# Hybrid attention and recurrence layer on one core: four instead of five of x's chunks turned on PE, the first stage in one written table of moves, the squares later, two weight copies merged

## The chip, the cores and the metric

The kernel runs on one core of one Trainium2 chip. The metric is the device time of one execution in microseconds (us), here the median of three runs. A core has five engines that each work through a row of instructions of their own in order: PE (matrix products), DVE (elementwise), ACT (elementwise with a function), POOL (a slower elementwise engine, and DMAs started by software) and SP, which in this kernel only starts DMAs. An engine waits for another by semaphores.

## The reference

One layer on x of 512 tokens x 2048 features, float32:

```python
def hybrid_layer(x, norm_w, w_in, ...):
    h = rms_norm(x, norm_w)
    proj = jnp.einsum('bsd,de->bse', h, w_in)            # 2048 -> 4608
    q, k, v, g_attn, xr, g_lru = jnp.split(proj, SPLITS, axis=-1)
    attn_out = attention_group(q, k, v, q_norm_w, k_norm_w)   # 8 heads, 2 for k and v, axial rope
    lru_out = lru_group(xr, conv_w, conv_b, ...)              # conv of 4 taps, gates, scan both ways
    mixed = jnp.concatenate([rms_norm(attn_out, attn_norm_w) * jax.nn.silu(g_attn),
                             rms_norm(lru_out, lru_norm_w) * jax.nn.silu(g_lru)], axis=-1)
    return x + jnp.einsum('bse,ed->bsd', mixed, w_out)
```

Each product is made in float32 accuracy from split operands: a high part (a cast) and a low part (the rest), three matmuls high x high, high x low and low x high.

## The kernel before, in words

All matrix work is matmuls of 128 x 128 weights with 512 columns. A projection takes 512 output columns at a time and runs over w_in in eight chunks of 256 rows: a chunk is one load `wr` of 512 KB (L206, by SP), two casts on ACT into `wh` (L218) and two subtractions on DVE into `wl` (L219), and 24 matmuls on PE (L153 to L155; L388 in the first chunks). In the text a chunk of the first stage is c=0 to c=7 and its weights w0 to w7.

The **first stage** projects the first half of the LRU input while x itself comes in: x also has eight chunks (256 features of all tokens, 512 KB), and PE needs each with the features on the partitions. Before, chunks 0 to 4 are turned by PE (`xturn`, L253, eight 128 x 128 transposes a chunk, then scaled and split by ACT and DVE). Chunks 5 to 7 go the other way: DVE turns blocks of 32 x 32 (`blocks`, L281), SP writes them to DRAM (`put_aside`, L289, here called D), reads them back in four pieces with the blocks in their places (`bring_back`, L296, called R), and ACT and DVE scale and split them (L338, L339, called V). Each chunk is also squared for the norm (`xsquare`): by DVE for the turned chunks (L272), by ACT for the others (L268).

Behind it come the second half of the LRU input, K and V together, two halves of Q, attention, the gates and the output product, with the recurrence woven between the projections. Where the text speaks of them: `hs` are the results of the recurrence (L558), their squares `hsq` (L567, one buffer) are added into `hsum` on DVE (L568); K, V (`kv`) and the Q tiles (`ev`) are evacuated by ACT (L596), their squares for the head norm (`sh`) are summed by ACT (L608), the root is taken by POOL, and DVE applies norm and rope (L613 to L622). K and Q are also turned by DVE blocks through DRAM (`uq` to `qd` to `lq`), K into `kt`.

What sets the order: PE's row is written by hand throughout. In the first stage SP's row is as well, and ACT's and DVE's until step (1, 2) (chunk 1, output tile 2); behind that, a scheduler places the instructions of ACT, DVE and SP by their priorities (`high_priority(AHEAD)`: as if written 600 instructions sooner) and by when it takes their operands to be ready. `moves` names what each step of the first stage brings, `issue_after` holds an instruction behind another. SP's row is one queue: what waits there holds up what stands behind.

Of the kernel before, what the change touches and what calls it, by code (L numbers as in the profile page):

```python
# [11 lines left out]
F32 = mybir.dt.float32  # L12
# [5 lines left out]
P = 128  # L18
# [31 lines left out]


B = 32
TURNED = 5
NQ = P // B


# [7 lines left out]
def hybrid_kernel(  # L64
# [53 lines left out]
    def nm(s):  # L118
        cnt[0] += 1
        return f"{s}_{cnt[0]}"  # L120
# [28 lines left out]
    def f(ap):  # L149
        return ap.bitcast(F32)  # L150
# [78 lines left out]

    xh, xl = [None] * KT, [None] * KT  # L230
    ssq = const([P, NT, KT // 2], "ssq")
    highs, x_parts, squared = {}, [], []

    def xload(c, nk=1):

        xc = b4(shape=(P, NT, 2 * P))
        for k in range(nk):
            ks = slice(k * 2 * P // nk, (k + 1) * 2 * P // nk)
            cs = slice(c * 2 * P + ks.start, c * 2 * P + ks.stop)
            nc.sync.dma_start(xc[:, :, ks], xf[:, cs].rearrange("(t p) d -> p t d", p=P))  # L240
            yield xc

    def behind(those):
        stack = ExitStack()
        for ins in those:
            stack.enter_context(tc.issue_after(ins))
        return stack

    def xturn(xc, kk, then=None):
        pt = mm()  # L250
        for t in range(NT):
            ks = slice(kk % 2 * P, (kk % 2 + 1) * P)
            nc.tensor.transpose(pt[:, t * P : (t + 1) * P], xc[:, t, ks], ident)  # L253
        if then:
            then()
        xh[kk], xl[kk] = x2(), x2()
        with behind(split_done[-1] if kk > 3 else ()):
            highs[kk // 2] = nc.scalar.activation(
                xh[kk], pt, AF.Identity, scale=nw[:, kk : kk + 1]
            ).ins  # L260
        nc.vector.scalar_tensor_tensor(
            xl[kk], pt, nw[:, kk : kk + 1], f(xh[kk]), op0=ALU.mult, op1=ALU.subtract
        )

    def xsquare(xc, c):
        for t in range(NT):
            if c >= TURNED:
                nc.scalar.activation(  # L268
                    xc[:, t, :], xc[:, t, :], AF.Square, accum_out=ssq[:, t, c : c + 1]
                )  # L270
                continue
            square = nc.vector.scalar_tensor_tensor(  # L272
                xc[:, t, :], xc[:, t, :], 1.0, xc[:, t, :], op0=ALU.mult, op1=ALU.mult,
                accum_out=ssq[:, t, c : c + 1],
            )
            if c == 1:
                squared.append(square.ins)

    def blocks(u, t, src):

        nc.vector.transpose(  # L281
            u[:, :, :, t, :].rearrange("p b k r -> p k b r"),
            src.rearrange("p (k b c) -> p k b c", k=2, c=B),
        )
# [15 lines left out]
    def in_order(v):  # L300
        return v.rearrange("p (t i r) -> p i t r", t=NT, i=NQ)

    def xchunk(c):
        with tc.high_priority(AHEAD):
            (xc,) = xload(c)
        yield
        if c < TURNED:
            with tc.high_priority(AHEAD):
                for k in range(2):
                    xturn(xc, 2 * c + k)  # L310
            if c == 2:
                yield
            with behind(split_done[2][1:] if c == 2 else ()):
                xsquare(xc, c)
            yield
            return
        u, back = (
            ring.tile([P, NQ, 2, NT, B], F32, name=nm("xu")) for ring in (aring, hring)
        )
        with tc.high_priority(AHEAD), tc.issue_after(squared[-1] if c == TURNED else split_done[3][1]):  # L320
            for t in range(NT):
                blocks(u, t, xc[:, t, :])
        yield
        with tc.high_priority(AHEAD):
            there = put_aside(u, "xd", KT // 2 - TURNED)
        with tc.issue_after(highs[TURNED - 1]):
            xsquare(xc, c)
        yield
        with tc.high_priority(AHEAD):
            bring_back(back, there)  # L330
        yield
        with tc.high_priority(AHEAD), behind(split_done[-1]):
            for k in range(2):
                kk = 2 * c + k
                xh[kk], xl[kk] = x2(), x2()
                hi, lo = (in_order(v) for v in (xh[kk], xl[kk]))
                v = back[:, :, k]
                nc.scalar.activation(v, v, AF.Identity, scale=nw[:, kk : kk + 1])  # L338
                x_parts[:] = nc.scalar.copy(hi, v).ins, nc.vector.tensor_sub(lo, v, f(hi)).ins  # L339
        yield  # L340

    last_pool = [None]

# [8 lines left out]
    def rows(dst, col, dg):  # L352

        shape = [P, NT, P]
        part = [const([P, NT], nm("part")) for _ in range(2)]
        parts = [dg() for _ in part]
# [12 lines left out]
        yield  # L369
# [537 lines left out]
    def first_sums():  # L907

        for m in range(NP + 1):
            if m < NP:  # L910
                copy_to(*((t3[g][m], block(m, 0, 2 * g)) for g in range(2)))
            if m:
                for g in range(2):
                    add_to(t3[g][m - 1], block(m - 1, 1, 2 * g))
            yield
        for m in range(NP):
            copy_to((t1[m], block(m, 0, 0)), (t2[m], t30[m]))
            yield

    def more_sums():  # L920
# [246 lines left out]
    with tc.high_priority():  # L1167
        xs, ws = xload(0, 2), wraw(w_in, 0, C_XR, 2)
        nc.scalar.dma_start(nw_st, norm_w.rearrange("(k p) -> k p", p=P))
        xc, raw = next(xs), next(ws)  # L1170
        next(xs), next(ws)
        table = const([P, 1], "table")
        nc.scalar.activation(table, ones[:, :1], AF.Exp)
        first = []

        def split_first():
            first.append(wsplit(raw, 0, nc.vector.tensor_copy))

        columns(nw, nw_st)
        xturn(xc, 0, split_first)  # L1180
        busy(WARM2)
    stats = xstats()
    chunks = [xchunk(c) for c in range(1, KT // 2)]

    raws = {}

    def fetch_x(c):
        with tc.high_priority(AHEAD):
            (raws[c],) = wraw(w_in, c * 2 * P, C_XR)

    def split_x(c):
        with tc.high_priority(AHEAD), behind(x_parts):
            given[c] = [wsplit(raws[c], k) for k in range(2)]

    moves = {
# [6 lines left out]
    }  # L1202

    def move(step):
        for name in moves.get(step, "").split():
            n = int(name[1])
            if name[0] == "x":
                next(chunks[n - 1])
            else:
                (fetch_x if name[0] == "w" else split_x)(n)  # L1210

    for step in proj_feat(C_XR, a1, first, given):
        if step is None:
            with tc.high_priority():
                first.append(wsplit(raw, 1, nc.vector.tensor_copy))
                xturn(xc, 1)
            xsquare(xc, 0)
            move(None)
            given[1] = wload(w_in, 2 * P, C_XR)
# [10 lines left out]
        if (c, e) in ((4, 3), (KT // 2 - 1, 0)):  # L1230
            with tc.high_priority(AHEAD), tc.issue_after(split_done[-1][1]):
                next(stats)

    s1.close()
    last_x = loads_done["lru"] = loads_done[nc.sync]
# [213 lines left out]
```

## Time and profile before

| | us |
|---|---|
| median of 3 runs | 627.53 (627.31 to 627.67) |
| span of the profiled execution | 625.3 |
| DVE busy | 494.8 |
| ACT busy | 353.2 |
| POOL busy | 101.7 |

The span runs from the first to the last instruction of the profiled execution. The views give no other time of that execution; the median of the runs stands 2.2 us above its span, and that is taken as what lies around it. A row of groups gives line, engine, operation, output and input, the count, the busy time and the mean in nanoseconds of one, and the idle time before with what ended it. A row of the timeline gives start, length, engine and line, the count of joined instructions, and in brackets the idle time of the engine before it, with the engine that ended it.

### The profile page before, as it was taken

How to read it: one execution, taken by the hardware profiler on the slowest of the kernel's cores; microseconds unless marked ns; L12 is line 12 of the kernel's file. 1: busy time of each engine (PE TensorE's matmuls, PEld its weight loads, DVE VectorE, ACT ScalarE, POOL GpSimd, SP SyncE). 2: the span in 40 equal slices, each digit the busy share in tenths (PEclk: the TensorE clock that was granted, in tenths of full speed). 3: DMA queues.
4: the chain of work that ended last, by engine and by line, in shares of the span. 5: the costliest groups of instructions: out<-in, count | busy, mean ns of one | idle time of the engine just before them, and what ended most of it. 6: DMA issues, size and time to landing. Idle time of an engine off the chain costs nothing.

```text
span 625.3 us, 8281 instructions
## 1 busy us (share of the span) xinstructions
PE 620.3 (99%) x2758; PEld 512.8 (82%) x2758; DVE 494.8 (79%) x796; ACT 353.2 (56%) x617; POOL 101.7 (16%) x134
## 2 busy tenths in 40 slices
PE   9999999999999999999999999999999999999997
PEld 7888888888888888888888888888888888888886
DVE  5967979986699875987887888549979866886886
ACT  3764899479945823545485448428445633443441
POOL 0000210112003531622123223100310101010010
PEclk9999999999999999999999999999999999999999
DMA  8878785859774599479658646923995677896262
GB/s 289 293 210 253 179 206 163 175 136 197 236 231 140 169 235 250 103 204 273 186 175 258 201 140 192 265 79 106 261 248 185 210 253 240 293 327 233 68 202 101
DMA packets 73595, 127.61 MB, mean 204 GB/s; under 512 B 6617, under 2 KB 29265, under 8 KB 73553
## 3 DMA queue, kind: packets, MB, share of 16 engines
q1 hardware_dynamic: 65664, 109.65, 56.7%
q0 software_dynamic: 7712, 17.31, 14.3%
q8 instruction: 21, 0.34, 0.2%
q14 instruction: 22, 0.17, 0.1%
q10 hardware_dynamic: 176, 0.14, 0.1%
HBM read 110.29 MB, written 37.75 MB: 237 GB/s over the span
## 4 chain that ended last, share of the span: by engine, by line
PE 99%; DVE 0%; issue 0%; POOL 0%; POOLq 0%
PE pj L153 20%; PE pj L154 20%; PE pj L155 20%; PE mm L1029 14%; PE pj L1029 11%; PE mm L155 3%; PE mm L154 3%; PE mm L153 3%; PE pj L388 2%; PE mm L253 1%; PE mm L1156 1%; PE mm L829 0%; PE mm L367 0%; DVE cb L1058 0%; PE mm L189 0%
## 5 line engine op out<-in xcount | busy, mean ns | idle before, releaser
L153 PE MATMUL pj<-x,wh 128*128 128x512 f32 x368 | 143.5, 390 | 0.0
L155 PE MATMUL pj<-x,wl 128*128 128x512 f32 x368 | 143.2, 389 | 0.0
L154 PE MATMUL pj<-x,wh 128*128 128x512 f32 x368 | 143.2, 389 | 0.0
L218 ACT CAST wh<-wr 128x512 fp32r<-128x512 f32 x142 | 84.9, 620 | 78.9 <-PE pj L154 31.2
L219 DVE TENSOR_TENSOR wl<-wr,wh 128x512 fp32r<-128x512 f32 x144 | 99.9, 724 | 19.7 <-ACT wh L218 18.6
L881 ACT CAST wh<-wr 128x1024 fp32r<-128x1024 f32 (+1 forms) x72 | 60.8, 862 | 75.7 <-PE mm L1029 34.6
L882 DVE TENSOR_TENSOR wl<-wr,wh 128x1024 fp32r<-128x1024 f32 (+1 forms) x72 | 68.8, 985 | 30.5 <-ACT wh L881 30.3
L155 PEld LDWEIGHTS pj<-x,wl 128*128 128x128 f32 x368 | 69.1, 188 | 14.5
L153 PEld LDWEIGHTS pj<-x,wh 128*128 128x128 f32 x368 | 69.1, 188 | 14.3
L154 PEld LDWEIGHTS pj<-x,wh 128*128 128x128 f32 x368 | 69.1, 188 | 14.3
L153 PE MATMUL pj<-wh,x 128*128 128x512 f32 x192 | 74.7, 389 | 0.0
L155 PE MATMUL pj<-wh,x 128*128 128x512 f32 x192 | 74.7, 389 | 0.0
L154 PE MATMUL pj<-wl,x 128*128 128x512 f32 x192 | 74.7, 389 | 0.0
L905 POOL DMA_DIRECT2D t<-in_w_out_dram x40 | 33.5, 891 | 156.6 <-DMA t<-in_w_out_dram 99.4
L1029 PE MATMUL mm<-wh,ml 128*128 128x512 f32 x126 | 49.0, 389 | 0.0
L1029 PE MATMUL mm<-wh,mh 128*128 128x512 f32 x126 | 49.0, 389 | 0.0
L1029 PE MATMUL mm<-wl,mh 128*128 128x512 f32 x126 | 49.0, 389 | 0.0
L155 PEld LDWEIGHTS pj<-wh,x 128*128 128x128 f32 x192 | 36.0, 188 | 7.6
L153 PEld LDWEIGHTS pj<-wh,x 128*128 128x128 f32 x192 | 36.0, 188 | 7.5
L154 PEld LDWEIGHTS pj<-wl,x 128*128 128x128 f32 x192 | 36.0, 188 | 7.4
L706 POOL TENSOR_SCALAR p<-p,sm 128x512 f32<-128x512 f32 x32 | 24.3, 762 | 89.4 <-DVE sm L705 89.4
L1029 PE MATMUL pj<-wl,mh 128*128 128x512 f32 (+1 forms) x100 | 38.5, 385 | 0.0
(201 smaller groups left out, 1053.6 us busy)
## 6 DMA issues: line engine op xcount, KB each, us to landing
wr<-in_w_in_dram SPq DMA_DIRECT2D x71, 512.0 KB, 5.1
wr<-in_w_out_dram SPq DMA_DIRECT2D x24, 512.0 KB, 5.1
t<-in_w_out_dram POOLq DMA_DIRECT2D x40, 256.0 KB, 6.9
wr<-t SPq DMA_DIRECT2D x40, 256.0 KB, 5.4
pd<-u SPq DMA_DIRECT2D x16, 512.0 KB, 3.0
pt<-pd SPq DMA_DIRECT2D x64, 128.0 KB, 3.6
t<-in_w_out_dram SPq DMA_DIRECT2D x24, 256.0 KB, 5.4
t<-t SPq DMA_DIRECT2D x16, 256.0 KB, 5.1
```

What stands on the lines that cost most here:

```text
L153: nc.tensor.matmul(acc, lh, rh, start=start, stop=False)
L154: nc.tensor.matmul(acc, lh, rl, start=False, stop=False)
L155: nc.tensor.matmul(acc, ll, rh, start=False, stop=stop)
L218: copy(hi, raw[:, k, :]).ins,
L219: nc.vector.tensor_sub(lo, raw[:, k, :], f(hi)).ins,
L253: nc.tensor.transpose(pt[:, t * P : (t + 1) * P], xc[:, t, ks], ident)
L388: nc.tensor.matmul(acc[e], w[:, e * P : (e + 1) * P], x_[2 * c + k], start=c == k == j == 0, stop=False,)
L706: last_pool[0] = nc.gpsimd.tensor_scalar(p, p, sm, 0.0, op0=ALU.mult, op1=ALU.add).ins
L881: nc.scalar.copy(hi[:, to], b)
L882: nc.vector.tensor_sub(lo[:, to], b, f(hi[:, to]))
L905: nc.gpsimd.dma_start(dst, src, accum_op=ALU.add)
L1029: nc.tensor.matmul(dst[s][:, es], lh[:, ts_], rh[:, es], start=i == ends_[0] and j == 0, stop=i == ends_[1] and j == 2,)
```

## The change

`TURNED` goes from 5 to 4: chunk 4 of x goes by DVE blocks and DRAM as chunks 5 to 7 did, so PE has eight transposes fewer, DVE four block transposes more, and SP one write and four reads. The generator `xchunk` with its `issue_after` holds is gone. In its place every act of the first stage has a letter (load, fetch weights, turn, half of a turn's split, squares, split of weights, blocks, put aside, bring back, split of a whole chunk, statistics), and one table says which stand at which step. ACT and DVE keep the written order until step (5, 3) instead of (1, 2). The squares of x6 and x7 are written late, at step (3, 2). In `first_sums` the copies of w_out's first rows into `t1` are joined two and two for m < 4.

```diff
-TURNED = 5
+TURNED = 4
...
         xh[kk], xl[kk] = x2(), x2()
-        with behind(split_done[-1] if kk > 3 else ()):
-            highs[kk // 2] = nc.scalar.activation(
-                xh[kk], pt, AF.Identity, scale=nw[:, kk : kk + 1]
-            ).ins
+        yield
+        nc.scalar.activation(xh[kk], pt, AF.Identity, scale=nw[:, kk : kk + 1])
+        yield
         nc.vector.scalar_tensor_tensor(
...
-    def xchunk(c):
...
+    def block_x(c):
+        units[c] = [ring.tile([P, NQ, 2, NT, B], F32, name=nm("xu")) for ring in (aring, hring)]
+        for t in range(NT):
+            blocks(units[c][0], t, chunk[c][:, t, :])
...
+    def whole_x(c):
+
+        for k in range(2):
+            v = units[c][1][:, :, k]
+            nc.scalar.activation(v, v, AF.Identity, scale=nw[:, 2 * c + k : 2 * c + k + 1])
+        for k in range(2):
+            kk = 2 * c + k
+            xh[kk], xl[kk] = x2(), x2()
+            hi, lo = (in_order(v) for v in (xh[kk], xl[kk]))
+            v = units[c][1][:, :, k]
+            nc.scalar.copy(hi, v)
+            nc.vector.tensor_sub(lo, v, f(hi))
...
+        firsts = w_out[:, :SEQ].rearrange("(m k p) e -> m k p e", k=2, p=P)[:, 0]
         for m in range(NP):
-            copy_to((t1[m], block(m, 0, 0)), (t2[m], t30[m]))
+            if m >= 4:
+                copy_to((t1[m], firsts[m]))
+            elif m % 2 == 0:
+                copy_to((t1[m : m + 2], firsts[m : m + 2]))
+            copy_to((t2[m], t30[m]))
             yield
...
     moves = {
-        None: "x1", (0, 2): "x1",
-        (1, 0): "x2", (1, 1): "x2", (1, 2): "x3 w2 s2 x2", (1, 3): "x3",
-        (2, 0): "x5 x4 x5", (2, 1): "x4 w3", (2, 2): "x6 x7", (2, 3): "w4 s3",
-        (3, 0): "x5 w5 x5 w6", (3, 1): "x6 x7 x6 x7", (3, 3): "s4 x5",
-        (4, 0): "x6 w7 x7", (4, 3): "s5 x6",
-        (5, 3): "s6 x7", (6, 3): "s7",
+        None: "Q0 Q0 L1 W1 S1 L2 L4 W2 L3",
+        (0, 2): "T1 H1 H1 L5 W3 B4 D4 L6 R4 W4",
+        (1, 0): "Q1 S2",
+        (1, 1): "Q1",
+        (1, 2): "T2 H2 H2 T3 H3 B5 D5 S3 H3 Q4 Q4",
+        (2, 0): "B6 D6 L7 R5 W5 Q5 Q5 V4",
+        (2, 2): "S4 Q2 Q2 B7 D7 R6 W6 R7 W7 Q3 Q3",
+        (3, 2): "V5 S5 Q6 Q6 Q7 Q7 Z0",
+        (4, 2): "V6 S6 Z0",
+        (5, 2): "V7 S7",
     }
...
-        if (c, e) == (1, 2):
+        if (c, e) == (5, 3):
             s2.close()
```

How the rows of the engines change is seen at three places. Names end in a number that tells one tile from the other; numbers differ by a few between the two kernels, and their lines by up to 3.

**ACT in the first stage**, from the split of chunk 5 on (`wh` from `wr`: weights of c=5 and c=6; L338, L335: the scale of V; L268, L267: squares). Before:

```order
L338 ACTIVATE xu_334<-xu_334,nw 128x4x128 x2
L339 CAST x_81_465<-xu_334 128x4x4x32
L268 ACTIVATE b_62_377,ssq<-b_62_377 128x256
L339 CAST x_83_470<-xu_334 128x4x4x32
L218 CAST wh_516<-wr_407 128x512
L218 CAST wh_520<-wr_407 128x512
L268 ACTIVATE b_62_377,ssq<-b_62_377 128x256 x3
L338 ACTIVATE xu_422<-xu_422,nw 128x4x128 x2
```

Of the change:

```order
L341 CAST x_83_466<-xu_329 128x4x4x32
L341 CAST x_85_470<-xu_329 128x4x4x32
L218 CAST wh_474<-wr_376 128x512
L218 CAST wh_478<-wr_376 128x512
L267 ACTIVATE b_40_250,ssq<-b_40_250 128x256 x4
L267 ACTIVATE b_68_370,ssq<-b_68_370 128x256 x4
L335 ACTIVATE xu_363<-xu_363,nw 128x4x128 x2
```

All eight squares of x6 and x7 now stand in one piece between the casts of w5 and the scale of chunk 6.

**ACT and DVE where K, V are done and the first half of Q is projected** (`wr_1882` before and `wr_1886` now are the weights of the fourth of that half's eight chunks; `kv` the evacuated K and V, `hs` the recurrence). ACT before:

```order
L546 ACTIVATE b_320_1685<-b_320_1685 128x1024
L218 CAST wh_1884<-wr_1882 128x512
L218 CAST wh_1888<-wr_1882 128x512
L218 CAST wh_1922<-wr_1920 128x512
L218 CAST wh_1926<-wr_1920 128x512
L218 CAST wh_1975<-wr_1973 128x512
L218 CAST wh_2021<-wr_2015 128x512
L608 ACTIVATE sh_1713,rr_1712<-kv_1674 128x128
```

ACT of the change, from where the sh and v of all of K and V have begun:

```order
L611 ACTIVATE sh_1731,rr_1730<-kv_1682 128x128
L566 ACTIVATE hsum<-hs_890 128x1024
L611 ACTIVATE sh_1733,rr_1730<-kv_1682 128x128
L570 ACTIVATE hsq_1999<-hs_1089 128x1024
L611 ACTIVATE sh_1738,rr_1737<-kv_1684 128x128
L611 ACTIVATE sh_1740,rr_1737<-kv_1684 128x128
L570 ACTIVATE hsq_2014<-hs_1449 128x1024
L570 ACTIVATE hsq_2041<-hs_1702 128x1024
L218 CAST wh_1888<-wr_1886 128x512
L218 CAST wh_1892<-wr_1886 128x512
L218 CAST wh_1925<-wr_1923 128x512
```

DVE of the change, at the same place, where before `wl_1885` and `wl_1889` stood ahead of the last two additions into hs:

```order
L571 TENSOR_TENSOR hsum<-hsum,hsq_2014 128x1024
L624 TENSOR_TENSOR kv_1684<-kv_1684,rk 128x256
L280 STREAM_TRANSPOSE uq_2059<-kv_1678 128x2x4x32
L625 TENSOR_TENSOR kv_1684<-kv_1684,sq_1762 128x256
L280 STREAM_TRANSPOSE uq_2059<-kv_1680 128x2x4x32
L571 TENSOR_TENSOR hsum<-hsum,hsq_2041 128x1024
L280 STREAM_TRANSPOSE uq_2059<-kv_1682 128x2x4x32
L280 STREAM_TRANSPOSE uq_2059<-kv_1684 128x2x4x32
L219 TENSOR_TENSOR wl_1889<-wr_1886,wh_1888 128x512
L219 TENSOR_TENSOR wl_1893<-wr_1886,wh_1892 128x512
```

The casts of that chunk moved behind the four squares of the recurrence and all of K's sums, and its subtractions behind K's norm, rope and block transposes and the additions into hsum.

**ACT at the start of the second half of Q** (`wr_2194` before, `wr_2196` now: its first chunk; `ev` the evacuated tiles of the first half). Before:

```order
L218 CAST wh_2070<-wr_2064 128x512
L218 CAST wh_2200<-wr_2194 128x512
L218 CAST wh_2196<-wr_2194 128x512
L608 ACTIVATE sh_1734,rr_1733<-kv_1680 128x128
L608 ACTIVATE sh_1736,rr_1733<-kv_1680 128x128
L218 CAST wh_2236<-wr_2234 128x512
L567 ACTIVATE hsq_2012<-hs_1445 128x1024
L218 CAST wh_2240<-wr_2234 128x512
L567 ACTIVATE hsq_2039<-hs_1698 128x1024
L218 CAST wh_2272<-wr_2270 128x512
L218 CAST wh_2276<-wr_2270 128x512
L596 ACTIVATE ev_2100<-pj_1764,rstd 128x512
```

Of the change:

```order
L599 ACTIVATE ev_2108<-pj_1771,rstd 128x512
L611 ACTIVATE sh_2126,rr_2121<-ev_2104 128x128
L611 ACTIVATE sh_2128,rr_2121<-ev_2104 128x128
L611 ACTIVATE sh_2133,rr_2132<-ev_2106 128x128
L611 ACTIVATE sh_2135,rr_2132<-ev_2106 128x128
L611 ACTIVATE sh_2137,rr_2132<-ev_2106 128x128
L611 ACTIVATE sh_2139,rr_2132<-ev_2106 128x128
L611 ACTIVATE sh_2144,rr_2143<-ev_2108 128x128
L611 ACTIVATE sh_2146,rr_2143<-ev_2108 128x128
L611 ACTIVATE sh_2148,rr_2143<-ev_2108 128x128
L611 ACTIVATE sh_2150,rr_2143<-ev_2108 128x128
L218 CAST wh_2198<-wr_2196 128x512
```

Three chunks of weights that were cast ahead of the first evacuation are now cast behind the last evacuation and all 16 sums; on DVE `wl_2199` likewise stands behind norm, rope and block transposes of the four tiles (L616 to L625, L280).

More of the change, by code (lines that the diff above doesn't have):

```diff
@@ L263, in xturn @@
         )
+        yield
     def xsquare(xc, c):
@@ L270, in xsquare @@
                 )
[L271 to L277, printed above, removed]
+            else:
+                nc.vector.scalar_tensor_tensor(
+                    xc[:, t, :], xc[:, t, :], 1.0, xc[:, t, :], op0=ALU.mult, op1=ALU.mult,
+                    accum_out=ssq[:, t, c : c + 1],
+                )
+            if t % 2:
+                yield
     def blocks(u, t, src):
@@ L301, in in_order @@
         return v.rearrange("p (t i r) -> p i t r", t=NT, i=NQ)
-    def xchunk(c):
[L304 to L340, printed above, removed]
@@ new lines, in hybrid_kernel, with load_x, turn_x, step_x @@
+    chunk, squares, halves, units = {}, {}, {}, {}
+    def load_x(c):
+        (chunk[c],) = xload(c)
+        squares[c] = xsquare(chunk[c], c)
+    def turn_x(c):
+        halves[c] = [xturn(chunk[c], 2 * c + k) for k in range(2)]
+        step_x(c)
+    def step_x(c):
+        for half in halves[c]:
+            next(half)
+    def square_x(c):
+        next(squares[c])
+    def block_x(c):
+        units[c] = [ring.tile([P, NQ, 2, NT, B], F32, name=nm("xu")) for ring in (aring, hring)]
+        for t in range(NT):
+            blocks(units[c][0], t, chunk[c][:, t, :])
@@ new lines, in aside_x, with back_x @@
+    def aside_x(c):
+        units[c][0] = put_aside(units[c][0], "xd", KT // 2 - TURNED)
+    def back_x(c):
+        bring_back(units[c][1], units[c][0])
+    def whole_x(c):
[9 more added lines that the diff above has]
+            nc.vector.tensor_sub(lo, v, f(hi))
@@ L355, in rows @@
         part = [const([P, NT], nm("part")) for _ in range(2)]
+        yield
         parts = [dg() for _ in part]
@@ L1179, in hybrid_kernel @@
         columns(nw, nw_st)
-        xturn(xc, 0, split_first)
+        drain(xturn(xc, 0, split_first))
         busy(WARM2)
+    squares[0] = xsquare(xc, 0)
     stats = xstats()
-    chunks = [xchunk(c) for c in range(1, KT // 2)]
     raws = {}
     def fetch_x(c):
-        with tc.high_priority(AHEAD):
-            (raws[c],) = wraw(w_in, c * 2 * P, C_XR)
+        (raws[c],) = wraw(w_in, c * 2 * P, C_XR)
     def split_x(c):
-        with tc.high_priority(AHEAD), behind(x_parts):
-            given[c] = [wsplit(raws[c], k) for k in range(2)]
-    moves = {
[6 rows of a table removed]
+        given[c] = [wsplit(raws[c], k) for k in range(2)]
+    acts = {
+        "L": load_x, "W": fetch_x, "T": turn_x, "H": step_x, "Q": square_x, "S": split_x,
+        "B": block_x, "D": aside_x, "R": back_x, "V": whole_x, "Z": lambda _: next(stats),
+    }
+    moves = {
[10 rows of a table added]
     }
     def move(step):
[L1205 to L1210, printed above, removed]
+        with tc.high_priority(AHEAD):
+            for name in moves.get(step, "").split():
+                acts[name[0]](int(name[1]))
     for step in proj_feat(C_XR, a1, first, given):
@@ L1215, in hybrid_kernel @@
                 first.append(wsplit(raw, 1, nc.vector.tensor_copy))
-                xturn(xc, 1)
-            xsquare(xc, 0)
+                drain(xturn(xc, 1))
             move(None)
-            given[1] = wload(w_in, 2 * P, C_XR)
             continue
@@ L1229, in hybrid_kernel @@
             columns(vec, vec_st)
-        if (c, e) in ((4, 3), (KT // 2 - 1, 0)):
-            with tc.high_priority(AHEAD), tc.issue_after(split_done[-1][1]):
-                next(stats)
+        if (c, e) == (KT // 2 - 1, 0):
+            next(stats)
     s1.close()
```

1 line of the change is left out of this document (removed).

## The prediction

> **What bounds the kernel now.** I read the busy times first, then DVE's share of each of 40 slices, the chain of work that ended last and the table of PE's waits, to see whether any engine but PE sets the end.
>
> ```profile
> PE 620.3 (99%) x2758; PEld 512.8 (82%) x2758; DVE 494.8 (79%) x796; ACT 353.2 (56%) x617; POOL 101.7 (16%) x134
> DVE  5967979986699875987887888549979866886886
> PE 99%; DVE 0%; issue 0%; POOL 0%; POOLq 0%
> PE mm L1156 <- POOL ones L161: 1.1, 1, 1.1
> ```
>
> PE is busy for 620.3 of 625.3 us, the chain is 99% PE, and the only wait that PE has is 1.1 us at the very start. So a microsecond of matrix work taken out can be worth a microsecond, and every wait that a changed order puts in front of PE is paid in full: nothing is idle that could take it back. DVE is at 79%, so work that is moved on DVE has little room. The span is 625.3 us and the median of the runs 627.53 us; the 2.2 us between them lie around the span, and I add my changes to 627.5.
>
> **The part that saves.** One chunk of x fewer is turned on PE: 8 transposes fewer (2750 matmul instructions for 2758).
>
> ```profile
> 22.77 1.04 PE L253 MATMUL mm<-ident,b 128*128 128x128 f32 x8
> 23.57 0.47 PE L153 MATMUL pj<-x,wh 128*128 128x512 f32 x1
> 23.88 0.39 PE L154 MATMUL pj<-x,wh 128*128 128x512 f32 x1
> 24.11 0.40 PE L155 MATMUL pj<-x,wl 128*128 128x512 f32 x1
> ```
>
> Eight transposes hold PE from 22.77 to 23.57, 0.80 us, and the matmul behind them takes 0.31 to the next start where the following one takes 0.23: 0.88 us in all. The saving is **0.9 us**, and no more can come from this part. The fifth chunk through DRAM adds four block transposes on DVE, one 512 KB write and four 128 KB reads. DVE is 5 tenths busy in its first slice of 15.6 us and has room for them; the transfers are in the next term. The merged t1 copies move the same bytes with two DMAs fewer: I cost them at nothing, hidden behind PE in a stage where no transfer is waited for.
>
> **The first stage: what comes late.** SP issues its transfers in one row, so the added write and reads stand ahead of weights. Ahead of the load of w5 now stand D4, D5, D6, R4, R5 and all of x. At the rate of the full queue the 19 transfers of 0.5 MB up to and including w5 take 27 us (1.44 us each at about 365 GB/s, an estimate from the row below), so w5 could be there at 29.5 us.
>
> ```profile
> wr<-in_w_in_dram SPq DMA_DIRECT2D x8, 512.0 KB, 5.8
> GB/s 369 366 374 366 349 348 374 370 351 363 354 389 414 401 182 43 169 265 148 127 391 416 414 180 98 249 196 184 367 250 198 62 23 21 119 363 281 259 257 236
> 25.08 1.76 SPq L296 DMA_DIRECT2D xu<-xd  x4
> 29.54 1.34 ACT L338 ACTIVATE xu<-xu,nw 128x512 f32<-128x512 f32 x2 [0.29 <-DMA xu<-xd]
> 28.75 0.41 ACT L268 ACTIVATE b<-b 128x256 f32<-128x256 f32 x1
> 38.10 1.34 ACT L338 ACTIVATE xu<-xu,nw 128x512 f32<-128x512 f32 x2 [3.53 <-DMA xu<-xd]
> 40.38 1.14 ACT L218 CAST wh<-wr 128x512 fp32r<-128x512 f32 x2
> 41.20 1.29 DVE L219 TENSOR_TENSOR wl<-wr,wh 128x512 fp32r<-128x512 f32 x2
> ```
>
> The first two rows are transfers from 10 to 50 us: a weight load lands 5.8 us after its issue, and in slices of 1 us the queue is full to 24 us, then well below. Each R has to wait for its D to land, and holds up the row. A 512 KB write in a full queue should take what a load takes, nearly 6; reads issued at 25.08 let ACT go at 29.54, 4.4 us later. With D4 issued at about 15 us (behind the blocks), R4 can go at about 20.5 and lands near 25, x7 and D5 follow, R5 goes at about 29 and lands at 33.5, and w5, right behind it, at about 36.3. PE wants c=5 at about 35.7 (it begins 5.7 us in, chunks of 24 matmuls and the transposes that are left), and a cast of 0.57 and a subtraction of 0.65 come first: PE is late by **1.4 us**, between 0 and 3. For c=6 the new order of ACT counts: the eight squares of x6 and x7 (8 x 0.41 = 3.3) stand between the casts of w5 and V6. From 37.4 (w5's casts done) that is 40.7, V6 takes 2.4 (1.25 for the scale, 1.03 for the copies, a gap), S6's first cast 0.6: 43.7, where PE would come at about 42.6. **1.2 us** more, between 0 and 1.7. So this stage gives -0.9 + 1.4 + 1.2 = +1.7 us, with ends at -0.9 (all hidden) and +3.8.
>
> **The large part: order behind the first stage.** From step (5,3) on, the scheduler chooses what ACT, DVE and SP do, and it chooses otherwise than before, far behind the edit: this is what the rows of order in the part on the change show. PE's own order there is unchanged.
>
> *First Q weights.* In before, the casts for the later chunks of Q's first half run just as PE releases the tiles.
>
> ```profile
> 173.49 1.30 ACT L218 CAST wh<-wr 128x512 fp32r<-128x512 f32 x2 [1.01 <-PE pj L155]
> 178.93 1.83 ACT L218 CAST wh<-wr 128x512 fp32r<-128x512 f32 x3 [4.13 <-PE pj L155]
> 179.41 0.39 PE L153 MATMUL pj<-wh,x 128*128 128x512 f32 x1
> 206.61 0.39 PE L153 MATMUL pj<-wh,x 128*128 128x512 f32 x1
> 183.87 0.69 DVE L558 TENSOR_TENSOR hs<-b 128x512 f32<-128x512 f32 x1
> 181.43 1.27 DVE L219 TENSOR_TENSOR wl<-wr,wh 128x512 fp32r<-128x512 f32 x2
> 197.41 0.42 DVE L622 TENSOR_TENSOR kv<-kv,sq 128x256 f32<-128x256 f32 x1
> 197.74 0.49 DVE L615 TENSOR_TENSOR sq<-kv,rk 128x128 f32<-128x128 f32 x2
> 198.14 0.42 DVE L663 TENSOR_TENSOR v<-kv,v 128x256 fp32r<-128x256 f32 x1
> 198.81 1.22 DVE L568 TENSOR_TENSOR hsum<-hsum,hsq 128x1024 f32<-128x1024 f32 x1
> 200.07 1.06 ACT L567 ACTIVATE hsq<-hs 128x1024 f32<-128x1024 f32 x1 [4.20 <-DVE hsum L568]
> 201.03 0.60 ACT L218 CAST wh<-wr 128x512 fp32r<-128x512 f32 x1
> ```
>
> The pair cast at 173.49 (wh_1884) is the one that PE's chunk at 179.41 starts with; five chunks of 24 matmuls later, at 206.61, the second Q half starts (27.2 us, 0.2267 us a matmul). In the changed order the same pair (wh_1888 there) stands behind the last square `hsq_2041`. That square needs the last hs, and its only buffer free: the row at 200.07 shows what that means, ACT stood 4.20 us until DVE had added the square before, and the cast came behind it. Now the chain by these durations. The last hs is done at 183.87 + 0.69 = 184.6; two pairs of wl, one of them at 181.43, are no longer ahead of it on DVE and take 1.2 each away (start to start): 182.1. Behind it come on DVE 11 small operations at 0.34 (197.41 to 197.74 and its like) and three pairs at 0.40 (197.74 to 198.14), 4.9 us, to 187.0; the first hsum addition, 1.14 to 188.1; four more small ones, 1.4 to 189.5; the second addition, to 190.7. Only then ACT may do the last square, 0.96 to 191.6, and the first cast, 0.6 to 192.2. DVE meanwhile does four small ones to 192.1, the third addition to 193.2, two block transposes (0.35 each) to 193.9, and the first wl, to 194.6. PE's second matmul needs wl: before it ran at 179.63, now at 194.6, **15.0 us** later. It is 13.5 if the small operations before the additions overlap better, and 17 if DVE waits for POOL's root as often as it did before.
>
> *Second Q half.* Here the casts were strewn among the evacuations; now they stand behind all of these on ACT, and on DVE behind norm and rope of all four tiles.
>
> ```profile
> 204.79 0.68 ACT L596 ACTIVATE ev<-pj,rstd 128x512 f32<-128x512 f32 x1
> 210.90 0.31 ACT L608 ACTIVATE sh<-ev 128x128 f32<-128x128 f32 x1
> 211.34 0.31 ACT L608 ACTIVATE sh<-ev 128x128 f32<-128x128 f32 x1
> 209.07 0.69 DVE L613 TENSOR_TENSOR ev<-ev,rr 128x512 f32<-128x512 f32 x1 [1.62 <-POOL rr L347]
> 209.80 0.76 DVE L615 TENSOR_TENSOR sq<-ev,rq 128x256 f32<-128x256 f32 x2
> 224.04 2.07 DVE L281 STREAM_TRANSPOSE uq<-ev 128x256 f32<-128x256 f32 x6
> ```
>
> PE ends the first half at 206.6 + 15.0 = 221.6; the four accumulators are complete 1.36 us apart (six matmuls), at 217.5 to 221.6. ACT evacuates the last by 222.3, then ten squares at 0.44 (210.90 to 211.34): 226.7, first cast done at 227.3. DVE needs longer: its first operation on ev came 4.28 us after the evacuation began (204.79 to 209.07), so 217.6 + 4.3 = 221.9; four tiles of 0.60 + 0.68 + 0.60 + 0.60 and four block transposes at 0.35 make 11.3, to 233.2; the first wl to 233.9. PE's second matmul would have run at 206.83 + 15.0 = 221.8: **12.1 us** late, 10 if the first tile's root comes sooner, 15 if DVE waits between the tiles.
>
> *K on its way back.* K is written to DRAM and read back into lq; kt, and then the sum of squares (kv) that PE spreads at L829 (L832 in the changed kernel), are made behind it.
>
> ```profile
> 208.89 1.29 SPq L296 DMA_DIRECT2D lq<-qd  x3
> 212.83 0.47 SPq L296 DMA_DIRECT2D lq<-qd  x1
> 217.22 1.15 ACT L652 CAST kt<-lq 128x512 fp32r<-128x512 f32 x2 [1.51 <-DMA lq<-qd]
> 236.53 0.62 PE L829 MATMUL mm<-kv,ones_r 128*128 128x512 f32 x2
> ```
>
> Before, lq was there 19 us ahead of the spread, 29.9 us behind the start of the half. Now the reads stand on SP behind copies and two more weight loads, one of which waits for a raw tile that is free only after the eighth pair of this half is split, 23 us into it. About 24.6 us into the half the last read goes out, 4.4 us later (212.83 to 217.22) it has landed, or 5.8 where it queues behind the weight load, and casts, subtraction and kv take 2.5: 31.5 to 32.9, where the spread is due at 29.9. I take **2.5 us**, with 0 and 8 as ends (8 if a second weight load has to land first).
>
> *PE after a long wait.* Before, PE never stops, so no row shows a restart; the nearest is the start.
>
> ```profile
> 1.13 2.53 PE L1156 MATMUL mm<-ones 128*128 128x256 bf16 x11 [1.13 <-POOL ones L161]
> 0.00:5.00 5.00, 3.87 (x18) 2.73 (x19) 0.35 (x2) 1.53 (x3) 1.13 (x10) 1.00 0.60 178
> ```
>
> Eleven matmuls of 256 columns take 0.23 each, as long as those of 512 columns take later: for that time at least, and some 4 us by the transposes and matmuls up to 5 us, PE runs at half its rate, though the granted clock in that window reads 1.00. If a wait of 12 to 15 us sets PE back in the same way, each costs half of some 3.9 us, 1.9 us; the bounds are 0 and 2.0. I take 1.9 twice, **3.8 us**, since the start is the one row there is.
> The Trainium skill, "TensorE: Matmul & The Clock Gate", Part 1, states that PE falls to half clock after an idle window of about 3.4 us and is back after about 3.4 busy ones; by its figure a long wait would cost an estimated 1.7 us, and the total 0.4 us less. The start in this trace agrees with the half rate; no run here shows a restart yet.
>
> **Sum.** +1.7 + 15.0 + 12.1 + 2.5 + 3.8 = +35.1 us: 627.5 + 35.1 = 662.6, **663 us**. The lower ends (-0.9, 13.5, 10, 0, 0) give +22.6, 650 us; the upper ones (3.8, 17, 15, 8, 4) +47.8, 675 us.
>
> **Rivals.**
> *All of it is hidden.* If the casts that PE needs were finished by 179.4 and 206.6 in spite of their place, only the transposes would count: 627.5 - 0.9 = 626.6 us, faster by 0.14%, or a little more if the first stage also loses gaps. For it speaks that before has no wait anywhere, with casts that end barely ahead of PE. It decides if DVE finishes the last hsum addition 15 us sooner than worked out, which the last hs at 182 us excludes unless ACT and DVE keep another order than the listing. Chance 0.04.
> *Only the first stage shows:* 627.5 + 1.7 = 629.2 us, if the Q weights' casts find cover but w5 and the squares don't. Chance 0.05.
> *One long wait instead of two:* the second half's casts are caught up because PE comes 15 us later anyway: 627.5 + 1.7 + 15.0 + 1.9 = 646 us. Against it, the wl of the second half stand behind work on the accumulators that PE itself finishes last. Chance 0.05.
> *Longer:* lq and the weights behind it come late by more than 8 us, or the half rate lasts: above 675 us. Chance 0.06.
>
> **How the numbers follow.** The forecast has 0.80, and the range 650 to 675 is that of its terms; outside are 0.20. A measurement of this kernel can tell some 0.2%, 1.3 us, from no change. Faster by more has 0.02 (half of the first rival, if the first stage also loses gaps), within 0.2% 0.03 (the other half and a little of the second), slower 0.95.
>
> **What would show it.** Right: PE's waits name ACT wh L218 and DVE wl L219 with one wait of about 12 us and a second part of 2, and again some 6 and 6; slices of PE with 0 to 5 tenths at about 180 to 195 and 221 to 234 us; ACT's casts behind a run of L570 and of L611 rows; matmuls of 512 columns 0.43 apart behind each. Wrong: no wait of PE over 5 us; PE's L153 of that chunk at 179 us as before; or the loss found in the first 50 us or in the last stage.

## The result, and the profile after

The changed kernel takes **679.57 us** (median of 5 runs, 678.74 to 680.61) where before takes 627.33 (627.22 to 627.67): a ratio of 1.0831, 95% interval 1.0818 to 1.0844. It is slower, as forecast, and by more: 52.2 us where 35.1 was forecast. 663 us was predicted, with 675 as the upper end.

The page of the changed kernel, in the parts shown of before (busy times; PE in 40 slices; the clock granted to PE; the chain that ended last), and its table of PE's waits (engine, line, who ended the wait, total, times, longest):

```profile
span 676.8 us, 8286 instructions
PE 630.3 (93%) x2750; PEld 517.3 (76%) x2750; DVE 495.1 (73%) x792; ACT 355.0 (52%) x627; POOL 102.4 (15%) x134
PE   9989999999739489299999999999999999999997
PEclk9999999999959779699999999999999999999999
PE 80%; DMA 6%; DVE 6%; ACT 4%; issue 1%; SPq 1%; POOL 1%; ACTq 0%; DVEq 0%; POOLq 0%
PE pj L153 <- ACT wh L218: 19.8, 4, 12.8
PE mm L832 <- ACT kv L824: 12.5, 1, 12.5
PE pj L154 <- DVE wl L219: 9.0, 2, 6.9
PE pj L155 <- DVE wl L219: 0.3, 2, 0.2
```

Every slice of PE behind 290 us is full again but the last, which reads 7 in before as well, so the loss lies ahead of it: waits of 41.6 us and a lower clock in four slices. PE's busy time rose by 10.0 us although it has eight transposes fewer: the same matmuls took longer. The timeline of PE has the waits at five places (start, length, and in brackets the idle time ahead with who ended it):

```profile
38.25 0.50 PE L153 MATMUL pj<-x,wh 128*128 128x512 f32 x1 [1.22 <-ACT wh L218]
44.76 0.50 PE L153 MATMUL pj<-x,wh 128*128 128x512 f32 x1 [0.34 <-ACT wh L218]
194.97 0.80 PE L153 MATMUL pj<-wh,x 128*128 128x512 f32 x1 [12.82 <-ACT wh L218]
197.79 0.80 PE L154 MATMUL pj<-wl,x 128*128 128x512 f32 x1 [2.02 <-DVE wl L219]
232.41 0.80 PE L153 MATMUL pj<-wh,x 128*128 128x512 f32 x1 [5.48 <-ACT wh L218]
240.15 0.80 PE L154 MATMUL pj<-wl,x 128*128 128x512 f32 x1 [6.94 <-DVE wl L219]
285.50 1.68 PE L832 MATMUL mm<-kv,ones_r 128*128 128x512 f32 x2 [12.51 <-ACT kv L824]
```

Taking the idle time off the starts, and comparing with before (179.41, 206.61, 236.53 in the prediction's rows), PE's lateness can be read at each place. It came to the first Q chunk at 182.15, 2.7 us late; to the second half at 226.93, 20.3 late; to the spread at 272.99, 36.5 late; at the end of the span it is 51.5 late. So the first stage cost 2.7 us, the first hand-over 17.6, the second 16.1, the third 15.0. Of the last three, 39.8 are idle time; the other 8.9 are the clock, as matmul after matmul behind each wait takes longer than in before.

ACT at the first hand-over shows the order that the rows of the change had told: two more squares, each held by DVE's addition, and only then five casts in one piece.

```profile
190.80 1.06 ACT L570 ACTIVATE hsq<-hs 128x1024 f32<-128x1024 f32 x1 [6.59 <-DVE hsum L571]
193.35 1.06 ACT L570 ACTIVATE hsq<-hs 128x1024 f32<-128x1024 f32 x1 [1.49 <-DVE hsum L571]
194.31 2.68 ACT L218 CAST wh<-wr 128x512 fp32r<-128x512 f32 x5
```

The third wait is another matter. The chain of waits there (start, length, what) ends in PE's spread at 286.39; before it stand the issue of a copy and two transfers one behind the other (the casts and subtractions of kt, from 283.79 to 285.73, are left out):

```profile
259.82 0.80 SPq L905
260.73 12.60 DMA t<-t
273.35 10.38 DMA lq<-qd
285.73 0.61 DVE kv L825
286.39 0.79 PE mm L832
```

By its timeline SP sends eight copies, a load and K's write in one go from 254 to 262 us; the last of the copies takes 12.6 us to land, and the last read of K, which SP sends only then, 10.4. In before the same reads had landed 4.4 us after the last was issued.

The clock, in windows around the first wait (columns: window, its length, the busy time and count of PE, PEld, DVE, ACT and POOL, then granted clock, DMA share, GB/s), and PE's timeline behind it:

```profile
178.00:190.00 12.00, 4.15 (x19) 3.10 (x17) 11.96 (x25) 2.99 (x8) 5.10 (x7) 0.78 0.10 38
190.00:200.00 10.00, 3.01 (x6) 2.11 (x7) 10.00 (x19) 4.70 (x7) 1.27 (x1) 0.50 0.06 8
200.00:205.00 5.00, 5.00 (x19) 3.98 (x18) 0.83 (x2) 0.62 (x1) 0.00 (x0) 0.82 0.73 251
200.94 0.63 PE L155 MATMUL pj<-wh,x 128*128 128x512 f32 x1
201.37 0.62 PE L153 MATMUL pj<-wh,x 128*128 128x512 f32 x1
202.06 0.40 PE L155 MATMUL pj<-wh,x 128*128 128x512 f32 x1
202.29 0.39 PE L153 MATMUL pj<-wh,x 128*128 128x512 f32 x1
```

Matmuls start 0.43 us apart (200.94 to 201.37) and from 202.06 on 0.23 apart: half rate for 4.3 us after PE goes on at 197.79.

### The profile page after: what moved, and what is told of

Its sections match the earlier page's. It is cut to its first block, busy times and chain, and to the rows that moved or that the text cites. A ratio compares the mean times of both kernels' runs of the same rounds, so it can differ in the third digit from the quotient of the medians.

```text
span 676.8 us, 8286 instructions
## 1 busy us (share of the span) xinstructions
PE 630.3 (93%) x2750; PEld 517.3 (76%) x2750; DVE 495.1 (73%) x792; ACT 355.0 (52%) x627; POOL 102.4 (15%) x134
## 4 chain that ended last, share of the span: by engine, by line
PE 80%; DMA 6%; DVE 6%; ACT 4%; issue 1%; SPq 1%; POOL 1%; ACTq 0%; DVEq 0%; POOLq 0%
PE pj L155 15%; PE pj L154 15%; PE pj L153 15%; PE mm L1037 13%; PE pj L1037 10%; PE mm L155 3%; PE mm L154 3%; PE mm L153 3%; DMA t<-t 2%; DMA lq<-qd 2%; PE pj L391 2%; DMA wr<-in_w_in_dram 1%; DVE wl L219 1%; DMA xd<-xu 1%; DMA xu<-xd 1%
## 5 line engine op out<-in xcount | busy, mean ns | idle before, releaser
L153 PE MATMUL pj<-wh,x 128*128 128x512 f32 x192 | 77.9, 406 | 18.3 <-ACT wh L218 18.3
L154 PE MATMUL pj<-wl,x 128*128 128x512 f32 x192 | 77.8, 405 | 9.0 <-DVE wl L219 9.0
L155 PE MATMUL pj<-wh,x 128*128 128x512 f32 x192 | 77.2, 402 | 0.0
L153 PEld LDWEIGHTS pj<-wh,x 128*128 128x128 f32 x192 | 37.9, 198 | 27.2 <-ACT wh L218 19.1
L154 PEld LDWEIGHTS pj<-wl,x 128*128 128x128 f32 x192 | 37.7, 196 | 18.0 <-DVE wl L219 10.0
L155 PEld LDWEIGHTS pj<-wh,x 128*128 128x128 f32 x192 | 37.7, 196 | 7.9
L1037 PE MATMUL pj<-wh,ml 128*128 128x512 f32 (+1 forms) x100 | 38.5, 385 | 0.0
```

Source lines behind the costliest of these rows:

```text
L153: nc.tensor.matmul(acc, lh, rh, start=start, stop=False)
L154: nc.tensor.matmul(acc, lh, rl, start=False, stop=False)
L155: nc.tensor.matmul(acc, ll, rh, start=False, stop=stop)
L1037: nc.tensor.matmul(dst[s][:, es], lh[:, ts_], rh[:, es], start=i == ends_[0] and j == 0, stop=i == ends_[1] and j == 2,)
```

## The experiments

**Which edit moves the later order: the copy's axes.** The change writes each merged copy with the pair as the first axis, 2 x 128 x 512; here the same two copies have the 128 rows first, 128 x 2 x 512.

```diff
-                copy_to((t1[m : m + 2], firsts[m : m + 2]))
+                copy_to(tuple(v[m : m + 2].rearrange("m p e -> p m e") for v in (t1, firsts)))
```

> The changed kernel with the two merged copies written with the 128 rows as the first axis and the pair as the second (same bytes, same two DMAs); nothing else is touched. In its rows the casts of Q's weights stand where they stood before the change. Theory A (the scheduler takes the copy as first written for a very long transfer and puts the weights' casts behind other work; the chip's own time for it is ordinary): all three long waits of PE go, 627.3 + 2.1 to 2.7 for the first stage = 629.4 to 630.0 us. Theory B (the merged copy is itself slow on the chip and holds up SP's row): waits stay, above 650 us. Theory C (the longer written order and the new table move the later work): about 680 us, as the change.

Measured: 631.41 us against 627.42 of before (ratio 1.0057, 1.0037 to 1.0077; single runs from 628.85 to 632.09), a little above the 629.4 to 630.0 of theory A. Its table of PE's waits has none above 1.2 us:

```profile
PE pj L153 <- ACT wh L218: 1.5, 2, 1.2
```

All three long waits are gone, 48.2 us with them. Theory C falls: the table and the written order are those of the change. Theory B is half true, since the swap changes the transfer as well as the order. The windows from 166 to 170 us, first of the change, where SP had last sent a merged copy (at 157.69) and one load (at 161.82), then of this run:

```profile
166.00:170.00 4.00, 4.00 (x20) 3.30 (x19) 1.68 (x3) 3.99 (x8) 0.00 (x0) 1.00 0.13 48
166.00:170.00 4.00, 4.00 (x19) 3.34 (x18) 1.33 (x3) 4.00 (x7) 0.00 (x0) 1.00 0.83 250
```

A share of 0.13 is about two of the 16 DMA engines, at 48 GB/s: as the change writes it, the merged copy is slow on the chip too. But PE does not wait for it. At the first hand-over ACT stands for DVE's additions, and DVE is busy for 21.96 of the 22 us from 178 to 200 (rows above); at the second the chain of waits runs over ACT's sums, POOL's root and DVE's norm. No transfer is in either, and SP's long waits there (22.7 us the longest) are for weight buffers that DVE has to free. So it is the order of the rows that makes PE wait, and the way the view is written that changes the order. Theory A's reason, that the scheduler takes the copy for a very long one, fits this, but no view shows what the scheduler reckons.

**The merged copies alone, in the kernel before.** Five chunks on PE, the old table, `copy_to` in pairs for m < 4 as in the diff of the change.

> The kernel before with the merged copies alone, as the change writes them; five chunks turned on PE and the old table of moves. Theory A: the same three waits of PE as in the change, 12.8 + 2.0, 5.5 + 6.9 and about 12.5 us, and no loss in the first stage: 627.3 + 52.2 - 2.7 = 676.8 us (674 to 679). Theory C: 627 us, no long wait.

Measured: 676.66 us, ratio 1.0779 (1.0758 to 1.0799), with the expected waits and none in the first stage:

```profile
PE pj L153 <- ACT wh L218: 18.3, 2, 12.8
PE mm L829 <- ACT kv L821: 12.0, 1, 12.0
PE pj L154 <- DVE wl L219: 9.0, 2, 6.9
```

49.2 of the 52.2 us come from making four small copies into two.

**One pair merged instead of two.**

```diff
-            if m >= 4:
+            if m >= 2:
                 copy_to((t1[m], firsts[m]))
```

> The changed kernel with only the first pair of copies merged, the other six single. In its rows the first Q weights stand behind the squares as in the change, those of the second half ahead of the evacuations as before. Theory A: the first wait only, 12.8 + 2.0 and about 2.7 for the clock: 630.0 + 17.5 = 647.5 us (643 to 652), the spread (L832) not late or under 3 us. If the second and third wait have a cause of their own beside the order, they stay: about 680 us.

Measured: 647.92 us in a single run, 0.4 from the expectation. PE waits at the first hand-over as in the change, and comes to the spread without a wait:

```profile
194.75 0.80 PE L153 MATMUL pj<-wh,x 128*128 128x512 f32 x1 [12.82 <-ACT wh L218]
197.57 0.79 PE L154 MATMUL pj<-wl,x 128*128 128x512 f32 x1 [2.02 <-DVE wl L219]
256.81 0.62 PE L832 MATMUL mm<-kv,ones_r 128*128 128x512 f32 x2
```

The first pair brings the first wait; the second and the third go away with the second pair, so the third doesn't come from the first.

**PE kept busy through all three waits.**

```diff
+            if (c0, c) in ((C_Q, 3), (C_Q + SEQ, 0)):
+                fill_in(100)
...
+        fill_in(100)
         spread(gbc, parts, NB * P)
```

> The changed kernel with 100 matmuls of 256 columns on constants, into a PSUM tile that nobody reads, put on PE ahead of each of the three places where it waits (at 0.11 us each about 11.4 us, so they fit into the 12.4 to 14.8 us of each wait). Theory A for the clock (PE runs at half rate for some 4 us after a long wait, and that costs 2 to 3 us each time): 679.6 - 6 to 8 = 672 to 674 us, the matmuls behind the waits 0.23 apart, and the granted clock near 1. If the rate does not fall because PE stood idle: 679.6 us or slightly more.

Measured: 678.88 us (ratio 1.0825, 1.0800 to 1.0850), within the noise of the change; the expectation of 672 to 674 missed. The profiled run shows why it could tell little: the filler (the added matmuls) ended 1.9 us ahead of the first cast and the rate fell all the same; and what was won behind the second wait went into the third, whose end is set by K's reads, not by PE. Its first stage also was 2 us later than that of the change. The granted clock rose from 0.964 to 0.987.

**The same with one wait, filled to its end.** One merged pair, and 140 matmuls ahead of the wait.

> The kernel with one merged pair (647.92 us, one long wait of PE of 12.8 + 2.0 us), with 140 matmuls of 256 columns on constants ahead of that wait (0.111 each by the run that was kept busy with 100 of them: 15.5 us, the whole wait). If PE's half rate comes from standing idle: the ten or so matmuls behind the wait are 0.23 apart instead of 0.43, 2.0 to 2.7 us less, 645.2 to 646 us at an equal first stage (which differed by up to 3 us from run to run). If the rate falls for another cause: 647.9 us, and half rate behind the wait as before.

```profile
181.79 15.46 PE L414 MATMUL mm<-ones 128*128 128x256 bf16 x140
197.00 0.48 PE L153 MATMUL pj<-wh,x 128*128 128x512 f32 x1
197.58 0.50 PE L154 MATMUL pj<-wl,x 128*128 128x512 f32 x1
197.92 0.39 PE L155 MATMUL pj<-wh,x 128*128 128x512 f32 x1
198.15 0.39 PE L153 MATMUL pj<-wh,x 128*128 128x512 f32 x1
```

Behind the filler (L414) matmuls start 0.23 apart at once. The profiled span is 643.5 us against 645.8 with one pair and no filler, 2.3 us less; PE comes to the wait at 181.79 here and at 181.93 there, so nearly all of it arises behind. The median of 4 runs is 646.73 (ratio 1.0307, 1.0293 to 1.0321), somewhat above the 645.2 to 646 expected and 1.2 less than the single run there. The spacing behind the wait decides it: the half rate comes from PE standing idle, and is paid on top of a wait.

**Is the third wait a heap of transfers?** The copies and additions from the third pair on are taken up a stage later.

```diff
-    fill = with_sums(both(), 3)
+    fill = with_sums(both(), 3, 0, 18)
```

> The changed kernel with the copies and additions of w_out from the third pair on put off into the gates' stage (the step at which they are taken up stops after 18 in the Q stage); merged copies and the places of the casts stay as in the change. Theory D (the third wait, 12.5 us at L832, is the queue of transfers: copies that SP held back while it stood come in one heap ahead of K's reads): waits of 12.8 + 2.0 and 5.5 + 6.9 stay, the third goes or is under 3 us, 679.6 - 12 to 15 = 665 to 668 us. If the third wait comes from the order of casts and raw tiles (as the prediction had it, 2.5 us by that alone) and not from the heap: it stays at 8 us or more, 675 us or above.

Measured: 672.63 us (ratio 1.0724, 1.0709 to 1.0739). PE's waits:

```profile
PE pj L153 <- ACT wh L218: 19.6, 3, 12.8
PE pj L154 <- DVE wl L219: 9.0, 2, 6.9
PE mm L153 <- ACT ph L729: 3.4, 2, 2.9
PE mm L154 <- DVE pl L729: 1.5, 2, 0.8
```

The wait at L832 is gone, as theory D has it, while the waits of both hand-overs stay to a tenth of a microsecond. The time came down by 7 instead of 12 to 15 us: the copies now meet the attention stage, where 4.9 us of waits and a clock of 0.93 between 320 and 370 us give a good part back.

**The first stage: D and R started by POOL.** From here on all kernels have the copies with swapped axes (631.41 us).

```diff
-        nc.sync.dma_start(aside_, u.rearrange("p b k t r -> p b (k t r)"))
+        queue.dma_start(aside_, u.rearrange("p b k t r -> p b (k t r)"))
...
+        units[c][0] = put_aside(units[c][0], "xd", KT // 2 - TURNED, nc.gpsimd)
```

> The change with the copies' axes swapped (no long waits, 631.4 us), and the writes and reads of x's blocks in the first stage started by POOL instead of SP. Theory E (the loss in the first stage is SP's row: reads that wait for their write hold up what stands behind them, and x's fifth chunk comes back late): no wait at c=5, at most the 1 us at c=6 that the squares cost, and the transposes' 0.9 us come out: 626.5 to 627.5 us, level with before or better by 0.1%. If the transfers are simply too many for the queue by then: the waits stay, 629 to 632 us.

Measured: 639.52 us (ratio 1.0196, 1.0176 to 1.0217); the expectation missed. POOL's timeline (D4, then R4):

```profile
15.43 0.71 POOL L288 DMA_DIRECT2D xd<-xu  x1 [13.72 <-DVE xu L280]
23.88 2.20 POOL L295 DMA_DIRECT2D xu<-xd  x4 [7.74 <-DMA xd<-xu]
```

From D4's issue by POOL to the first read it took 8.4 us (5.3 by SP in the change, 15.34 to 20.64), so the round trip got longer, and PE waited 4.6 and 5.3 us in this stage. This is no test of SP's row; it only shows that POOL's queue is the worse one here.

**Four squares instead of eight ahead of V6.**

```diff
-        (3, 2): "V5 S5 Q6 Q6 Q7 Q7 Z0",
-        (4, 2): "V6 S6 Z0",
-        (5, 2): "V7 S7",
+        (3, 2): "V5 S5 Q6 Q6",
+        (4, 2): "V6 S6 Q7 Q7 Z0",
+        (5, 2): "V7 S7 Z0",
```

> The change with the copies' axes swapped, and the squares of x7 moved from before V6 to behind S6, so that four instead of eight stand between the casts of w5 and V6. As the prediction had it, the eight squares make c=6 late by 1.0 us: that wait goes (four squares are 1.65 us, more than it), 1 us less than 631.4 in the median (629 where the first stage is quick). If the reads of chunk 6 come late in any case: the wait stays at 0.5 to 1 us and the time too.

Measured: 630.80 us (ratio 1.0060, 1.0045 to 1.0076): 0.6 below, not to be told from nothing. ACT's timeline, first of this run, then of the one with the axes alone:

```profile
42.88 1.14 ACT L218 CAST wh<-wr 128x512 fp32r<-128x512 f32 x2 [0.34 <-DMA wr<-in_w_in_dram]
```

```profile
43.48 1.13 ACT L218 CAST wh<-wr 128x512 fp32r<-128x512 f32 x2
```

The casts of c=6 come 0.6 us sooner and then wait for w6: the squares were ahead of that load by only this much. PE had no wait at c=6 here, but partly because it came later (its matmuls ran at half rate behind the wait at c=5).

**w4 ahead of R4.** SP's timeline in the change has nothing between x6's load at 15.73 and R4, the first row here; the second is R5.

```profile
20.64 1.76 SPq L295 DMA_DIRECT2D xu<-xd  x4
28.74 1.74 SPq L295 DMA_DIRECT2D xu<-xd  x4
```

```diff
-        (0, 2): "T1 H1 H1 L5 W3 B4 D4 L6 R4 W4",
+        (0, 2): "T1 H1 H1 L5 W3 B4 D4 L6 W4 R4",
```

> The change with the copies' axes swapped, and on SP the load of w4 moved from behind the four reads R4 to ahead of them; one swap of neighbours in the table. Theory F (in the first stage SP stands from 15.7 to 20.6 us while R4 waits for its write, with a load behind it that could go; what comes behind, D5, R5 and w5, is late by that): w4 goes out at about 16, D5 and R5 some 0.5 to 1.5 us sooner, the wait at c=5 (1.2 us, which in some runs also costs 1.7 us of half rate) is under 0.4 us; with what is left at c=6 the median is 627.3 - 0.9 + 0.3 to 1.0 = 626.7 to 627.4 us, against 631.4 without the swap. If the queue itself is what is late (as many bytes, whatever their order): the wait stays above 1 us and the median at 630 or more.

SP's timeline of this run (w4's load, R4, R5) and the one wait of PE left in it above 0.2 us:

```profile
16.27 1.05 SPq L206 DMA_DIRECT2D wr<-in_w_in_dram  x1
20.66 2.33 SPq L295 DMA_DIRECT2D xu<-xd  x4
27.82 1.75 SPq L295 DMA_DIRECT2D xu<-xd  x4
43.83 0.50 PE L153 MATMUL pj<-x,wh 128*128 128x512 f32 x1 [0.61 <-ACT wh L218]
```

Measured: 628.87 us (11 runs; ratio 1.0029, 1.0020 to 1.0037), 2.5 below the run without the swap (1.8 by the two ratios). R5 goes out at 27.82 instead of 28.74 and the wait at c=5 is gone, as theory F has it; the median still missed its 626.7 to 627.4. What is left in this profile: 1.1 us around c=6, 0.7 at c=5, where each cast comes just in time and PE takes short steps, and 0.5 at the start. The transposes' 0.9 us don't pay for it.

**Three moves in the table** (w4 ahead of R4, w6 ahead of R6, part of x7's squares and the statistics behind S6).

> As the run with w4 first, and two more moves: w6 ahead of R6, with D7 behind both, and two of x7's four squares (and the statistics) from before V6 to behind S6. Theory F: nothing waits at c=5 and c=6, the transposes' 0.9 us come out whole: 626.4 to 626.8 us, faster than before by 0.1%. If c=6 is late for a cause of its own (R6's reads): a wait of 0.5 us there, 627 us; if D7 is now too late for c=7, a wait at 48 us of up to 2 us.

Measured: 630.17 us (ratio 1.0042, 1.0030 to 1.0055); missed. No wait above 0.2 us is left in the first stage of the profiled run, but PE waits 1.2 us for ACT at L529 in the recurrence. Why the moves bring that wait was not followed up. No version tried beats the kernel before.

## Why the prediction was right or wrong, point by point

- **Transposes, 0.9 us.** Right. The matmuls at 20.23 and 23.88 of before, ahead of and behind the eight transposes, stand at 20.78 and 23.50 in the change: 0.55 late becomes 0.38 early, 0.93 us.
- **First stage, +1.7 us:** 2.7 in the profile. Matmul by matmul, PE is 0.38 early ahead of c=5, 1.51 late behind its start and 2.58 late behind that of c=6: c=5 cost 1.9 us (1.4 forecast), c=6 1.1 (1.2 forecast). The prediction's own terms give 1.8 for c=5 (36.3 + 0.57 + 0.65 against 35.7) and 1.1 for c=6 (43.7 against 42.6), so its sums were slightly off, and the size at c=5 was about right by luck: the prediction had w5 land last, but ACT sat 6.46 us for R5 and w5's casts stand behind V5 on ACT. The swap of w4 and R4 showed R5's way through SP's row as the cause. At c=6 the squares ahead of V6 count as argued, but only by some 0.6 us; behind that the load of w6 is the limit. Not foreseen: 0.6 us of half rate more at the start in this profile, and in other runs half rate after the wait at c=5.
- **First hand-over, 15.0 us:** 12.82 + 2.02 = 14.84 us. The chain by hand (hs, two additions on DVE, the last square, the cast; then wl) stands as written, each step some 2.6 us later, as PE is.
- **Second half, 12.1 us:** 5.48 + 6.94 = 12.42 us. Right.
- **K on its way back, 2.5 us:** 12.51. **This is the step that failed, by its size.** The prediction put the last read out "about 24.6 us into the half" and let it land 4.4 to 5.8 us later, from rows of an undisturbed queue. It went out 46.4 us after PE had come to the half (226.93 to 273.35), of which the second wait is 12.4. SP and PE had stood through both waits, the copies that would have gone out meanwhile came in one heap, and SP had to see a copy landed (12.6 us) before the last read went out, which took 10.4. With the copies put off, the wait was 0, so the order of casts and raw tiles, which gave the 2.5, cost nothing by itself. The rival "longer" named the place, at a chance of 0.06.
- **Half rate, 3.8 us:** 2.7 + 3.7 + 2.5 = 8.9. The mechanism was right and was shown by the filled wait; but the term was too small twice over: the third wait was not counted, and each costs more than the 1.9 of the start, since the half rate lasted 4.3 us behind the first wait and 6.1 behind the second. By the Trainium skill, "TensorE: Matmul & The Clock Gate", Part 1, PE falls to half clock after an idle window of about 3.4 us and is back after about 3.4 busy ones, an estimated 1.7 us a wait. Here it cost 2.5 to 3.7 a wait, and a gap between matmuls of 1.8 us at c=5 (in the run with the squares apart) was enough to bring it, while gaps of 1.5 to 2.0 in four others did not. The measurement decides.
- **The cause of the changed order** was left open in the prediction ("far behind the edit"), which put the merged copies at nothing. It is the view of these copies, 49.2 us by itself, not the extended written order or the table.
- **The sum:** 2.7 + 14.8 + 12.4 + 12.5 + 8.9 = 51.3 of the 51.5 us by which the span grew, where 35.1 was forecast. Of the difference 10.0 are K's, 5.1 the clock's and 1.0 the first stage's.
- **Rivals:** all hidden (626.6) and first stage only (629.2) are excluded by the waits; the second is close to what the change is without the view (631.41). One wait instead of two (646) is what a single merged pair gives.

## What to carry to other kernels

When a scheduler places instructions, compare the rows of every engine behind an edit, even one that touches no more than a copy's shape: here the order of a copy's axes moved the casts on ACT and the subtractions on DVE, and PE paid at places far from the edit. The length of a wait, worked out by hand, is only part of its price: the transfers that stood still come in a heap, and the next reader of the queue pays again; and the clock has to come back. A saving of 0.9 us on the engine that is the bound was not worth 1 MB more of transfers in a stage whose loads come just in time.

## What the runs showed of the hardware that was not expected

The half rate after a gap depends on more than its length: gaps of 1.74, 1.77 and 3.39 us between matmuls at c=5 were followed by some 3.5 us of matmuls 0.43 apart, gaps of 1.54, 1.60, 1.61 and 1.95 were not. The time with the axes alone varies by 3.2 us over five runs, at a granted clock of 0.997 where it is above 631 us and of 0.999 where it is below 630. The half rate at c=5 may be why, but a trace shows only one of the five. The granted clock of a window reads 1.00 at the start, where 256-column matmuls took 0.23 us each, as at half rate; in the filled wait they took 0.11 (140 in 15.46 us).
